# mLSTM outputs set aside in DRAM and the gate pairs woven into fewer column groups, in a hybrid encoder layer

## The chip, the cores and the metric

One Trainium2 chip, one core of it. The metric is the device time of one execution in microseconds, median of several runs. Times of single instructions come from one profiled execution.

## The reference

One layer over 256 rows of 2048 channels, float32: a SwiGLU feed-forward (2048 to 5632) with a residual and a layer norm; a mixer; a second feed-forward; a gated embedding. The change lies in the mixer:

```python
proj = x @ w_in                                   # 11272 columns
mq, mk, mv, mo, mi, mf, sq, sk, sv, ga, gb = _split_cols(proj)
q_m, k_m = split(silu(_causal_conv([mq, mk], conv_w)))
h   = _mlstm_chunkwise(q_m, k_m * 256**-0.5, mv, log_i, log_f)   # 4 heads of 256
y_m = head_norm(h) * sigmoid(mo)
y_sb = _stick_breaking(sq, sk, sv)                # 8 heads of 128
merged = sigmoid(ga) * (y_m @ w_up_m) + sigmoid(gb) * (y_sb @ w_up_sb)
return merged @ w_out
```

## The kernel before

**The work.** 256 rows are two halves `t` of 128. A product with a weight is cut into groups of 512 columns; a group runs over the weight's rows in pairs of 128. `group` makes one unit for each 256 rows of weight and each half `t`: six matmuls of 512 columns (L1194 to L1196), since each float32 operand is split into a high and a low part (hi x hi, hi x lo, lo x hi). So one weight tile is loaded once by the SP queue (`raw`, L1116), split once by ScalarE (high part, L1143) and VectorE (low part, L1147), and used by two units.

The pair of gates `ga` and `gb` is computed in another way. `seven` makes seven products in place of eight, Strassen's way, over sums of weight tiles: of each step of 512 rows a tile `t` is loaded, split, then grown by a DMA that adds another part of the weight to it (`grow`, L337, on GpSimd's queue), split again, and so on, until its fourth use; two more sums are made by VectorE (`plus`, L342). Here each split serves one unit only. `gates7(g)` makes such a group of four steps, 28 units, for each of the four column groups g; results are collected in two fixed banks, `seeded`.

**The order of the work.** Nothing is scheduled by a compiler: the program is a list of units, and `weave` puts the 28 x 4 = 112 units of the gates (with 20 blanks, `chained`) evenly between the units of `main`. Main holds the column groups of k, v, mo, q, k, v, mo (16 units each), six groups of stick-breaking columns (`sq0 + first * DS`, 16 units each, the last one of 256 columns), and six up halves of 8 units (`ups(g, half)`: half 0 is y_m times `w_up_m`, half 1 y_sb times `w_up_sb`, for g = 0, 1, 2): 256 units in all. The up products of g = 3 follow behind the weave.

Work that is no unit runs as a generator in `Sched`, put into the order after so many microseconds of planned TensorE time (`DELAY`): convolution, gate scans, the heads of mLSTM (`mlstm(h)`) and stick breaking (`stick(h)`), transposes (`sb_turn`), the derived forms of the activations that the seven products read (`form_turn`, with delay "form1" for the mixer's input).

**Memory.** One pool of 44 pages of 4 KB a partition serves raw tiles, split tiles, activations and most else. `room` holds two limits: how many raw tiles may be loaded and not yet free, and how many weights may be split ahead. Functions in main change it, `rooms(n)` the first alone, as the order reaches them; it begins at RAW_MIX = 8 and SPLIT_MIX = 4. A tile counts as raw until the last weight that is made of it has been split, for `t` of a pair its fourth. The output of mLSTM, transposed and split, is `ymT`: four tiles (head pair c, half t) of one page each, written by `split_psum` at the end of `mlstm` and read by the up products of half 0. They stay in their pages from the head that writes them until the last up product.

Of the kernel before, what the change touches and what calls it, by code (L numbers as in the profile page):

```python
# [13 lines left out]
P = 128  # L14
# [27 lines left out]


DELAY = {
    "gb": 12.0, "form": 14.0, "form1": 20.0, "ln_turn": 3.4, "ln_step": 1.2, "ln_low": 2.6, "h": 8.0, "silu": 6.0, "late": 9.0, "rest": 1.2, "mt": 3.2,
    "sbt": 4.6, "g0": 3.0, "g1": 4.0, "g2": 12.0, "cv0": 1.0, "cv1": 6.0, "turn": 3.5, "cv2": 1.3,
    "m0": 3.0, "m1": 0.6, "m2": 1.2, "m3": 4.6, "m4": 4.6, "s0": 6.6, "s1": 6.7, "s2": 4.0,
}

# [131 lines left out]
def kernel(  # L181
# [31 lines left out]
    def drop(n=1):  # L213
        temps[0] -= n
# [4 lines left out]
    def big(shape=(P, 1024)):  # L219
        return page_pool.tile(list(shape), F32, name="big", tag="page")  # L220

    pages, held, room = [0], [0], [RAW_MIX, SPLIT_MIX]

    def act_tile():
        pages[0] += 1
        return page_pool.tile([P, 2, 4, P], F32R, name="actT", tag="page")
# [163 lines left out]
    def rooms(*n):  # L390
        return lambda: room.__setitem__(slice(0, len(n)), n)
# [399 lines left out]
        return done  # L791

    ymT, ysbT = ActT(act_tile), ActT(act_tile)

    def diag(tl):
        return tl[:, 0:512].rearrange("q (a s) -> q a s", s=S)[:, :, 0:P]

    def mlstm(h):
        yield from wait("gates", ("qk", 0, h), ("qk", 1, h), ("v", 0, h // 2), ("v", 1, h // 2))
        d = temp()  # L800
        ps = misc([P, S])
        nc.tensor.matmul(ps[:], st["sel"][:, h], st["M"], start=True, stop=True)
        for s in range(2):
            activate(d[:, 256 * s:256 + P * s], ps[:, P * s:], ACT.Exp, scale=-1.0,
                                 bias=st["a"][:, s, h:h + 1])
        nc.gpsimd.affine_select(diag(d), diag(d), pattern=[[0, 2], [1, P]], compare_op=ALU.is_ge,
                                fill=0.0, base=0, channel_multiplier=-1)
        yield DELAY["m0"]
        q, k = st["qk", h][:, 0], st["qk", h][:, 1]
        ps = misc([P, 3 * P])  # L810
        for s in range(2):
            for b in range(2):
                nc.tensor.matmul(ps[:, 256 * s:256 + P * s], k[:, b, s * P:(s + 1) * P], q[:, b, s * P:],
                                 start=(b == 0), stop=(b == 1))
        nc.vector.scalar_tensor_tensor(out=d[:, 0:3 * P], in0=ps[:], scalar=DM ** -0.5, in1=d[:, 0:3 * P],
                                       op0=ALU.mult, op1=ALU.mult)
        yield DELAY["m1"]
        mv = small.tile([P, TT, 2], F32, name="hmv", tag="hmv")
        r = small.tile([P, TT], F32, name="hr", tag="hr")
        hs = temp().rearrange("q (t e) -> q t e", t=TT)  # L820
        for t in range(TT):
            ps = misc([P, DM + 1])
            for s in range(t + 1):
                off = s * 256 + (t - s) * P
                nc.tensor.matmul(ps[:], d[:, off:off + P], st["v", s, h // 2][:, h % 2], start=(s == 0), stop=(s == t))  # L825
            nc.vector.tensor_scalar(out=r[:, t:t + 1], in0=ps[:, DM:], scalar1=-1.0, scalar2=st["em"][:, t, h:h + 1],
                                    op0=ALU.mult, op1=ALU.max)
            nc.vector.tensor_tensor(out=r[:, t:t + 1], in0=ps[:, DM:], in1=r[:, t:t + 1], op=ALU.max)
            nc.vector.reciprocal(out=r[:, t:t + 1], in_=r[:, t:t + 1])
            yield DELAY["turn"]  # L830
            activate(hs[:, t], ps[:, 0:DM], ACT.Copy, scale=r[:, t:t + 1])
            yield DELAY["m2"]
        drop()
        for t in range(TT):
            stats = small.tile([P, 6], F32, name="hst", tag="hst")
            nc.vector.bn_stats(out=stats[:], in_=hs[:, t])
            nc.vector.bn_aggr(out=mv[:, t], in_=stats[:])
        rstd = small.tile([P, TT, 1], F32, name="hrs", tag="hrs")
        activate(rstd[:], mv[:, :, 1:2], ACT.Sqrt, bias=eps[:, 0:1])
        yield DELAY["m3"]  # L840
        yield from wait(("mo", 0, h // 2), ("mo", 1, h // 2))
        nc.vector.reciprocal(out=rstd[:], in_=rstd[:])
        for t in range(TT):
            nc.vector.tensor_scalar(out=hs[:, t], in0=hs[:, t], scalar1=mv[:, t, 0:1], scalar2=rstd[:, t],
                                    op0=ALU.subtract, op1=ALU.mult)
            nc.vector.tensor_tensor(out=hs[:, t], in0=hs[:, t], in1=st["mo", t][:, h * DM:(h + 1) * DM], op=ALU.mult)
        yield DELAY["m4"]
        for t in range(TT):
            ps = misc([P, 2, P])
            for b in range(2):  # L850
                nc.tensor.transpose(ps[:, b], hs[:, t, b * P:(b + 1) * P], ident[:])
            dst = ymT.get(h // 2, t)
            bs = slice(2 * (h % 2), 2 * (h % 2) + 2)
            split_psum(dst[:, 0, bs], dst[:, 1, bs], ps[:])
            ymT.mark(h // 2, t, 2)
        drop()

    def stick(h):
# [44 lines left out]
    head = group(w_in, range(0, D, 2 * P), 0, COL, x1T, qk_done(0, 0))  # L903
    program.extend(skewed(head[:SKEW]) + flat(head[SKEW:]))
    program.extend(columns(4096, 2 * HM + 2 * DS, gates_done))
    main = [rooms(10)] + columns(1024, COL, qk_done(1, 0)) + [rooms(8)]
    for g in range(2):
        if g:
            main += columns(COL, COL, qk_done(0, 1)) + [rooms(8)] + columns(1024 + COL, COL, qk_done(1, 1))
        else:  # L910
            main.append(load_norm_m)
        main += columns(2048 + g * COL, COL, v_done(g))
        main.append(lambda g=g: sched.spawn(in_sequence([mlstm(2 * g), mlstm(2 * g + 1)])))
        main += columns(3072 + g * COL, COL, mo_done(g))
    for first, n in ((2, 4), (8, 4), (16, 4), (12, 4), (20, 4), (6, 2)):
        main += columns(sq0 + first * DS, n * DS, lambda ps, t, f=first, n=n: sb_columns(ps, t, f, n))
        if first in (2, 20):
            main.append(rooms(11 if first == 2 else 6))
        if first == 16:
            main.append(rooms(8))  # L920
            main.append(lambda: [sched.spawn(in_sequence([stick(a), stick(a + 2), stick(a + 4), stick(a + 6)]))
                                 for a in (0, 1)])

# [55 lines left out]
    def merge_turn(g, t):  # L979
        transposed(gt[g, t], mergedT, g, t)  # L980
        return
        yield
# [3 lines left out]
            return flat(group(w_up_sb, range(0, HS * DS, 2 * P), g * COL, COL, ysbT, up_done(g, 1)))  # L986
        return flat(group(w_up_m, range(0, HM * DM, 2 * P), g * COL, COL, ymT, up_done(g, 0)))

    for half in range(2):
        for g in range(3):  # L990
            main += ups(g, half) + [rooms(8)]
    program.extend(weave(main, chained([gates7(g) for g in range(4)])))
    program.append(rooms(10, 6))
    program.append(lambda: [sched.spawn(merge_turn(g, t), 1.0 + 2.0 * g + t) for g in range(3) for t in range(TT)])
    program.append(lambda: sched.spawn(refill(), 14.0))
    program.extend(ups(3, 0) + ups(3, 1))
# [237 lines left out]
```

## Time and profile before

| | us |
|---|---|
| median of 3 runs (2218.99 to 2222.85) | 2220.16 |
| the profiled execution | 2221.91 |
| its span in the trace | 2220.2 |
| TensorE busy in the span | 2184.8 |
| VectorE, ScalarE, GpSimd busy | 1789.1, 1336.0, 228.8 |

The first feed-forward ends near 700 us, the mixer's woven part lies between about 740 and 1280, the second feed-forward and the embedding fill the rest. PE is TensorE, DVE VectorE, ACT ScalarE, POOL GpSimd, SP the queue that issues most loads. Matmuls are pipelined, so that a row lasts longer (0.39 us) than the distance from one start to the next (0.23 us). In a list of waits the columns are who waited for whom, microseconds in total, times, the longest.

### The profile page before, as it was taken

What the parts mean: (1) busy time and instruction counts of PE and PEld (TensorE: products, weight loads), DVE (VectorE), ACT (ScalarE), POOL (GpSimd) and SP (SyncE); (2) the same over time, 40 slices, a digit from 0 to 9 for tenths busy, and PEclk for the clock granted to TensorE, in tenths of its full rate; (3) what the DMA queues carried; (4) which work ended last, traced back from release to release, by engine and by line L of the source; (5) the groups of instructions that cost most, each with busy time, mean ns of one, the idle gap of its engine ahead of it and who ended that gap; (6) DMA issues with size and microseconds to landing.
All of it is one profiled execution on the core that took longest, in us unless ns stands there. A gap on an engine that the chain in (4) does not pass through costs nothing.

```text
span 2220.2 us, 27770 instructions
## 1 busy us (share of the span) xinstructions
PE 2184.8 (98%) x9972; PEld 1806.4 (81%) x9972; DVE 1789.1 (81%) x1967; ACT 1336.0 (60%) x1599; POOL 228.8 (10%) x201
## 2 busy tenths in 40 slices
PE   9999999999999999999998999999999999999999
PEld 7888888888887878778886888888888888888878
DVE  6889988888897878767655786599898989889884
ACT  6556656666575566665665554556665666666562
POOL 3111011110100011000111000011101110100000
PEclk9999999999999999999998999999999999999999
DMA  9899889987992878859575785579879998989652
GB/s 346 219 255 268 258 243 287 278 250 211 272 350 72 227 199 229 227 173 286 159 199 159 256 276 203 195 182 320 248 232 270 288 251 253 260 253 305 223 165 74
DMA packets 273194, 522.86 MB, mean 236 GB/s; under 512 B 16512, under 2 KB 25632, under 8 KB 272800
## 3 DMA queue, kind: packets, MB, share of 16 engines
q1 hardware_dynamic: 229248, 435.10, 57.9%
q0 software_dynamic: 43808, 85.99, 21.6%
q8 instruction: 78, 1.28, 0.2%
q14 instruction: 60, 0.49, 0.1%
HBM read 516.83 MB, written 4.19 MB: 235 GB/s over the span
## 4 chain that ended last, share of the span: by engine, by line
PE 92%; DVE 3%; ACT 2%; DMA 1%; issue 1%; DVEq 0%; SPq 0%; ACTq 0%
PE mm L1195 25%; PE mm L1196 25%; PE mm L1194 25%; PE seeded L1195 5%; PE seeded L1196 5%; PE seeded L1194 5%; DVE split L1147 2%; PE ms L267 1%; DMA raw<-in_w_in_dram 1%; ACT split L1143 1%; DMA raw<-in_w_up_m_dram 0%; PE ms L452 0%; PE ms L863 0%; PE ms L825 0%; DVE temp L761 0%
## 5 line engine op out<-in xcount | busy, mean ns | idle before, releaser
L1147 DVE TENSOR_TENSOR split<-raw,split 128x1024 fp32r<-128x1024 f32 (+2 forms) x1061 | 1242.7, 1205 | 221.2 <-ACT split L1143 208.0
L1143 ACT CAST split<-raw 128x1024 fp32r<-128x1024 f32 (+2 forms) x1061 | 1069.8, 1038 | 507.2 <-PE mm L1195 138.2
L1194 PE MATMUL mm<-split,actT 128*128 128x512 f32 (+2 forms) x2640 | 1027.9, 389 | 2.7 <-ACT big L1050 2.4
L1195 PE MATMUL mm<-split,actT 128*128 128x512 f32 (+2 forms) x2640 | 1017.1, 385 | 7.1 <-DVE split L1147 7.0
L1196 PE MATMUL mm<-split,actT 128*128 128x512 f32 (+2 forms) x2640 | 1016.7, 385 | 2.3 <-DVE actT L272 2.3
L1195 PEld LDWEIGHTS mm<-split,actT 128*128 128x128 f32 x2640 | 497.7, 189 | 106.8 <-DVE split L1147 11.6
L1196 PEld LDWEIGHTS mm<-split,actT 128*128 128x128 f32 x2640 | 497.0, 188 | 102.4 <-DVE actT L272 3.2
L1194 PEld LDWEIGHTS mm<-split,actT 128*128 128x128 f32 x2640 | 497.4, 188 | 100.1 <-ACT big L1050 3.3
L337 POOL DMA_DIRECT2D raw<-in_ffn_w_dram x128 | 154.7, 1219 | 1181.1 <-DVE split L1147 923.5
L342 DVE TENSOR_TENSOR raw<-raw 128x1024 f32<-128x1024 f32 x160 | 195.0, 1218 | 28.9 <-DMA raw<-in_w_in_dram 18.7
L1195 PE MATMUL seeded<-split,actT 128*128 128x512 f32 x480 | 187.9, 391 | 6.5 <-DVE split L1147 6.5
L1194 PE MATMUL seeded<-split,actT 128*128 128x512 f32 x480 | 189.1, 394 | 2.0 <-ACT split L1143 2.0
L1196 PE MATMUL seeded<-split,actT 128*128 128x512 f32 x480 | 187.5, 391 | 0.0
L568 DVE SCALAR_TENSOR_TENSOR xres<-mm,xres 128x512 f32<-128x512 f32 x160 | 108.9, 685 | 21.9 <-PE mm L1196 21.9
L1195 PEld LDWEIGHTS seeded<-split,actT 128*128 128x128 f32 x480 | 90.6, 189 | 25.9 <-DVE split L1147 7.9
L1194 PEld LDWEIGHTS seeded<-split,actT 128*128 128x128 f32 x480 | 90.4, 188 | 20.6 <-ACT split L1143 2.5
L1196 PEld LDWEIGHTS seeded<-split,actT 128*128 128x128 f32 x480 | 90.4, 188 | 18.9
L269 ACT CAST actT<-ms 128x512 fp32r<-128x512 f32 x60 | 35.2, 588 | 66.6 <-PE ms L267 65.0
L337 POOL DMA_DIRECT2D raw<-in_w_in_dram x32 | 38.7, 1208 | 310.5 <-DVE split L1147 302.7
L272 DVE TENSOR_TENSOR actT<-ms,actT 128x512 fp32r<-128x512 f32 x60 | 40.9, 685 | 24.7 <-ACT actT L269 14.3
L239 ACT ACTIVATE temp<-mm 128x512 f32<-128x512 f32 (+1 forms) x38 | 21.8, 574 | 57.9 <-PE mm L1196 57.8
L235 ACT ACT_TABLE_LOAD x35 | 44.9, 1283 | 0.6
(152 smaller groups left out, 706.8 us busy)
## 6 DMA issues: line engine op xcount, KB each, us to landing
raw<-in_ffn_w_dram SPq DMA_DIRECT2D x527, 512.0 KB, 8.1
raw<-in_w_in_dram SPq DMA_DIRECT2D x168, 512.0 KB, 4.8
raw<-in_ffn_w_dram POOLq DMA_DIRECT2D x128, 512.0 KB, 9.3
raw<-in_w_in_dram POOLq DMA_DIRECT2D x32, 512.0 KB, 7.7
raw<-in_w_out_dram SPq DMA_DIRECT2D x32, 512.0 KB, 5.8
raw<-in_w_ple_gate_dram SPq DMA_DIRECT2D x24, 512.0 KB, 4.9
raw<-in_w_up_m_dram SPq DMA_DIRECT2D x16, 512.0 KB, 5.4
raw<-in_w_up_sb_dram SPq DMA_DIRECT2D x16, 512.0 KB, 5.6
```

The source lines that it names most:

```text
L235: nc.scalar.preload_act_table_set(table[0])
L267: nc.tensor.transpose(ps[:, k], src[:, k * P:(k + 1) * P], ident[:])
L269: nc.scalar.copy(dst[:, 0], ps[:])
L272: nc.vector.tensor_tensor(out=dst[:, 1], in0=ps[:], in1=dst[:, 0], op=ALU.subtract)
L337: nc.gpsimd.dma_start(out=raw.tile[:, :, :cols], in_=src.src, accum_op=ALU.add)
L342: nc.vector.tensor_tensor(out=a.tile[:, :, :cols], in0=a.tile[:, :, :cols], in1=b.tile[:, :, :cols], op=ALU.add)
L568: nc.vector.scalar_tensor_tensor(out=xs, in0=ps, scalar=0.5, in1=xs, op0=ALU.mult, op1=ALU.add)
L1143: nc.scalar.copy(hi[:, ks], r[:, ks])
L1147: nc.vector.tensor_tensor(out=lo[:, ks], in0=r[:, ks], in1=hi[:, ks], op=ALU.subtract)
L1194: nc.tensor.matmul(ps, hi, w[0][:, k, :u.cols], start=first, stop=False, skip_group_check=u.onto)
L1195: nc.tensor.matmul(ps, hi, w[1][:, k, :u.cols], start=False, stop=False, skip_group_check=u.onto)
L1196: nc.tensor.matmul(ps, lo, w[0][:, k, :u.cols], start=False, stop=last, skip_group_check=u.onto)
```

## The change

It does four things.

1. **mLSTM's outputs go to DRAM.** When a tile of `ymT` has both its heads, `away(c, t)` stores it on GpSimd's queue (512 KB), after a delay of 6 us, and its page is given back. `back`, put into main four units ahead of the first up half, takes four new pages and loads the tiles again, on the same queue.
2. **The pairs are woven into less.** The three halves 1 of g = 0, 1, 2 leave main and follow behind the weave; main has 232 units in place of 256, among which the same 112 units of the pairs are spread.
3. **More raw tiles are loaded ahead** at most places of main, and six weights are split ahead in the head of the mixer in place of four (from the first unit of main on it is four again).
4. **Two delays:** the forms of the mixer's input come 10 us later ("form1"), the transposes of stick-breaking columns 1.4 us later ("sbt").

```diff
-    "gb": 12.0, "form": 14.0, "form1": 20.0, ...
-    "sbt": 4.6, ... "turn": 3.5, "cv2": 1.3,
+    "gb": 12.0, "form": 14.0, "form1": 30.0, ...
+    "sbt": 6.0, ... "turn": 3.5, "away": 6.0, "cv2": 1.3,
...
-    pages, held, room = [0], [0], [RAW_MIX, SPLIT_MIX]
+    pages, held, room = [0], [0], [RAW_MIX, 6]
...
+    aside = {(c, t): dram_pool.tile([P, 2, 4, P], F32R, name=f"aside{c}{t}") for c in range(2) for t in range(TT)}
+
+    def away(c, t):
+        nc.gpsimd.dma_start(out=aside[c, t][:], in_=ymT.tiles[c, t][:])
+        pages[0] -= 1
+        return
+        yield
+
+    def back():
+        for c in range(2):
+            for t in range(TT):
+                ymT.tiles[c, t] = act_tile()
+                nc.gpsimd.dma_start(out=ymT.tiles[c, t][:], in_=aside[c, t][:])
...
             ymT.mark(h // 2, t, 2)
+            if h % 2:
+                sched.spawn(away(h // 2, t), DELAY["away"])
...
-    main = [rooms(10)] + columns(1024, COL, qk_done(1, 0)) + [rooms(8)]
+    main = [rooms(10, 4)] + columns(1024, COL, qk_done(1, 0)) + [rooms(8)]
...
-            main += columns(COL, COL, qk_done(0, 1)) + [rooms(8)] + columns(1024 + COL, COL, qk_done(1, 1))
+            main += [rooms(9)] + columns(COL, COL, qk_done(0, 1)) + [rooms(9)] + columns(1024 + COL, COL, qk_done(1, 1))
...
         if first in (2, 20):
-            main.append(rooms(11 if first == 2 else 6))
+            main.append(rooms(12 if first == 2 else 10))
         if first == 16:
-            main.append(rooms(8))
+            main.append(rooms(11))
...
-    for half in range(2):
-        for g in range(3):
-            main += ups(g, half) + [rooms(8)]
+    main.insert(len(main) - 4, back)
+    for g in range(3):
+        main += ups(g, 0) + [rooms(12)]
     program.extend(weave(main, chained([gates7(g) for g in range(4)])))
     program.append(rooms(10, 6))
+    for g in range(3):
+        program.extend(ups(g, 1))
```

In the lists below, a line number of the changed kernel is 13 to 17 higher than that of the same statement before. Three places of the order:

The SP queue, at the loads of the last stick-breaking columns (`128x2x256`) and of the first up weights, before:

```order
L1116 DMA raw<-in_w_in_dram 128x2x512 x120
L1116 DMA raw<-in_w_in_dram 128x2x256
L1116 DMA raw<-in_w_in_dram 128x2x512 x2
L1116 DMA raw<-in_w_in_dram 128x2x256
L1116 DMA raw<-in_w_in_dram 128x2x512 x2
L1116 DMA raw<-in_w_in_dram 128x2x256 x2
L1116 DMA raw<-in_w_in_dram 128x2x512 x2
L1116 DMA raw<-in_w_in_dram 128x2x256 x4
L1116 DMA raw<-in_w_up_m_dram 128x2x512 x9
```

and now:

```order
L1133 DMA raw<-in_w_in_dram 128x2x512 x127
L1133 DMA raw<-in_w_in_dram 128x2x256 x6
L1133 DMA raw<-in_w_in_dram 128x2x512
L1133 DMA raw<-in_w_in_dram 128x2x256
L1133 DMA raw<-in_w_in_dram 128x2x512
L1133 DMA raw<-in_w_in_dram 128x2x256
L1133 DMA raw<-in_w_up_m_dram 128x2x512
L1133 DMA raw<-in_w_in_dram 128x2x512
L1133 DMA raw<-in_w_up_m_dram 128x2x512 x2
```

Loads of 512 columns of `w_in` are the pairs' there. Before, six of them stand among the eight narrow loads, and then nine up weights follow without one; now seven more of them stand ahead of the narrow loads, six narrow ones come in a row, and the pairs' loads alternate with the up weights.

GpSimd's queue between the last accumulating load of the mixer (L337) and the end of stick breaking, whose masks are the AFFINE_SELECT rows, before:

```order
L337 DMA raw<-in_w_in_dram 128x2x512 [waits DMASW4_49,DMASW0_49,DVE_49]
L881 AFFINE_SELECT temp<-temp 128x2x128 [waits Activation_49] x2
L337 DMA raw<-in_w_in_dram 128x2x512 [waits DMASW5_49,DMASW1_49,DVE_49]
L872 AFFINE_SELECT temp<-temp 128x2x128 [waits DVE_49,PE_49]
L872 AFFINE_SELECT temp<-temp 128x2x128 [waits DVE_49,PE_49,Activation_49]
```

and now:

```order
L337 DMA raw<-in_w_in_dram 128x2x512 [waits DMASW5_49,DMASW1_49,DVE_49]
L887 AFFINE_SELECT temp<-temp 128x2x128 [waits DVE_49,PE_49] x2
L806 DMA actT<-aside_94 128x1024 [waits DMAHW5_49,DVE_49,PE_49]
L806 DMA actT<-aside_95 128x1024 [waits DMAHW3_49,DMAHW5_49,DVE_49,Activation_49]
L806 DMA actT<-aside_96 128x1024 [waits DMAHW6_49,PE_49]
L806 DMA actT<-aside_97 128x1024 [waits PE_49]
L896 AFFINE_SELECT temp<-temp 128x2x128 [waits Activation_49] x2
```

The four reloads (L806) stand behind two masks that wait for VectorE, and two masks stand behind them. The DMASW and DMAHW names are semaphores of earlier DMAs.

TensorE at the end of the gates' columns (`128x264`) and at the first up half, before:

```order
L1196 MATMUL mm<-split,actT 128x264
L674 MATMUL ms<-ident,temp 128x128 [waits Activation_49]
L674 MATMUL ms<-ident,temp 128x128
L1194 MATMUL mm<-split,actT 128x512
L1195 MATMUL mm<-split,actT 128x512 [waits DVE_49]
```

and now, first the gates' end, then the first up half:

```order
L1213 MATMUL mm<-split,actT 128x264
L1211 MATMUL mm<-split,actT 128x512 [waits Activation_49]
...
L702 MATMUL ms<-ident,gst 4x128 [waits PE_49,Activation_49]
L702 MATMUL ms<-ident,gst 4x128 [waits Activation_49]
...
L1213 MATMUL mm<-split,actT 128x256
L1211 MATMUL mm<-split,actT 128x512 [waits Activation_49]
...
L1211 MATMUL mm<-split,actT 128x512 [waits DMASW6_49,PE_49,Activation_49]
...
L1211 MATMUL mm<-split,actT 128x512 [waits DMASW7_49,PE_49]
```

L674 is `sb_turn`, L702 the transposes of `gates`. Where the transposes stood right behind the gates' columns, 18 matmuls of 512 columns stand now, and the first thing of the gates that TensorE needs is `gst`. In the up half two units wait for the reloads (DMASW6 and DMASW7), six matmuls apart.

More of the change, by code (lines that the diff above doesn't have):

```diff
@@ L44 @@
 DELAY = {
-    "gb": 12.0, "form": 14.0, "form1": 20.0, "ln_turn": 3.4, "ln_step": 1.2, "ln_low": 2.6, "h": 8.0, "silu": 6.0, "late": 9.0, "rest": 1.2, "mt": 3.2,
-    "sbt": 4.6, "g0": 3.0, "g1": 4.0, "g2": 12.0, "cv0": 1.0, "cv1": 6.0, "turn": 3.5, "cv2": 1.3,
+    "gb": 12.0, "form": 14.0, "form1": 30.0, "ln_turn": 3.4, "ln_step": 1.2, "ln_low": 2.6, "h": 8.0, "silu": 6.0, "late": 9.0, "rest": 1.2, "mt": 3.2,
+    "sbt": 6.0, "g0": 3.0, "g1": 4.0, "g2": 12.0, "cv0": 1.0, "cv1": 6.0, "turn": 3.5, "away": 6.0, "cv2": 1.3,
     "m0": 3.0, "m1": 0.6, "m2": 1.2, "m3": 4.6, "m4": 4.6, "s0": 6.6, "s1": 6.7, "s2": 4.0,
```

## The prediction

> **What bounds the kernel now.** I read the page first: the busy times and the chain that ended last.
>
> ```profile
> PE 2184.8 (98%) x9972; PEld 1806.4 (81%) x9972; DVE 1789.1 (81%) x1967; ACT 1336.0 (60%) x1599; POOL 228.8 (10%) x201
> PE 92%; DVE 3%; ACT 2%; DMA 1%; issue 1%; DVEq 0%; SPq 0%; ACTq 0%
> ```
>
> TensorE is busy for 2184.8 of 2220.2 us and carries 92% of the chain. The change removes no matmul, so it can only win where TensorE stands idle (35.4 us in all) or runs slowly after standing idle. Where that is, the windows tell (columns: length, busy time of PE, PEld, DVE, ACT and POOL, granted clock, DMA share, GB/s):
>
> ```profile
> 0.00:700.00 700.00, 694.79 (x3119) 574.06 (x3120) 601.72 (x615) 429.11 (x475) 91.65 (x79) 1.00 0.88 261
> 725.00:750.00 25.00, 22.27 (x142) 20.04 (x141) 18.49 (x33) 16.07 (x27) 2.41 (x2) 0.93 0.82 225
> 750.00:1150.00 400.00, 393.23 (x1770) 320.91 (x1768) 296.86 (x373) 252.01 (x314) 45.78 (x43) 1.00 0.75 212
> 1150.00:1175.00 25.00, 20.66 (x95) 17.42 (x94) 12.31 (x13) 13.80 (x21) 1.21 (x1) 0.86 0.54 136
> 1175.00:1200.00 25.00, 22.03 (x132) 18.86 (x130) 16.16 (x19) 15.82 (x21) 7.12 (x8) 1.00 0.71 182
> 1200.00:1225.00 25.00, 20.50 (x82) 15.94 (x82) 13.08 (x18) 12.44 (x21) 1.68 (x2) 0.86 0.57 156
> ```
>
> Before 700 us, idle time is 5.2 us in 700. The three windows from 1150 to 1225, the last stick-breaking columns and the first up half, have 4.34 + 2.97 + 4.50 = 11.8 us idle in 75, and in two of them the clock is down to 0.86. DVE and ACT are *less* busy there than elsewhere, and the DMA engines too: nobody is short of throughput, everybody waits for one thing. The chain of waits of that stretch (start, length, what) names it:
>
> ```profile
> 1158.82 7.21 DMA raw<-in_w_in_dram
> ...
> 1168.57 0.80 PE seeded L1195
> 1169.37 0.43 PE seeded L1196
> 1169.79 0.43 PE seeded L1194
> ...
> 1173.92 4.93 DMA raw<-in_w_in_dram
> 1178.98 1.23 DVE raw L342
> ...
> 1196.19 10.43 DMA raw<-in_w_up_m_dram
> 1206.69 1.06 ACT split L1143
> ```
>
> All three stalls begin with a raw weight tile that was asked for too late. The groups of the mixer say how late is late (issue to landing, median):
>
> ```profile
> raw<-in_w_in_dram SPq DMA_DIRECT2D x164, 512.0 KB, 4.8
> raw<-in_w_in_dram POOLq DMA_DIRECT2D x32, 512.0 KB, 7.7
> raw<-in_w_up_m_dram SPq DMA_DIRECT2D x12, 512.0 KB, 6.5
> raw<-in_w_up_sb_dram SPq DMA_DIRECT2D x8, 512.0 KB, 6.1
> raw<-in_w_in_dram SPq DMA_DIRECT2D x8, 264.0 KB, 2.8
> ...
> kept<-xres POOLq DMA_DIRECT2D x2, 1024.0 KB, 5.6
> raw<-in_w_in_dram SPq DMA_DIRECT2D x8, 256.0 KB, 4.6
> ```
>
> How far ahead the loads run follows from `room`. These rows are of 640 to 1260 us, in which the SP queue loads 164 + 12 + 8 + 8 + 8 = 200 raw tiles of the mixer, one in 3.1 us. A seven-product group of four steps keeps its four `t` tiles from product 1 to product 4, and they count as raw. Where `rooms(6)` holds, behind the columns of `first == 20`, two places are left for all else: 2 x 3.1 = 6.2 us of lead, less than the 6.5 us that an up weight takes in the median and than the 7.21 and 10.43 us of the chain.
>
> **The change part by part.** *Rooms (term A).* Behind the same columns the limit is 10 and then 12 in place of 6 and 8: six to eight free places, 19 to 25 us of lead, more than 10.43. The order agrees: loads of the narrow last columns no longer alternate with the pair's. So the stalls of 1150 to 1225 should nearly go; what is late next there is the reload of term R. Their price is the idle 11.8 us plus what the slow clock costs. After a gap matmuls start 0.42 us apart (1169.37 to 1169.79), at full clock 0.23:
>
> ```profile
> 1139.97 0.39 PE L1194 MATMUL mm<-split,actT 128*128 128x512 f32 x1
> 1140.20 0.39 PE L1195 MATMUL mm<-split,actT 128*128 128x512 f32 x1
> ...
> 1161.28 0.28 PE L1196 MATMUL mm<-split,actT 128*128 128x256 f32 x1
> 1161.40 0.28 PE L1194 MATMUL mm<-split,actT 128*128 128x256 f32 x1
> ```
>
> A clock of 0.86 over 25 us is a shortfall of 3.5 us of full speed, 7.0 for two windows, part of it inside the idle time. So A is worth 11.8 to 18.8 us; I take 17 as what is there, since the slow pitch shows beyond the gaps, and 16 as what goes, leaving 1 for small waits that stay. The unfavourable end is 9: that only the two stalls of 1158 to 1183 go (idle 4.34 + 2.97, and half the clock's 3.5).
>
> *Seven-product units packed denser (no term).* 132 side places go over 232 units of main where they went over 256. With the two split rows and the sum row
>
> ```profile
> L1147 DVE TENSOR_TENSOR split<-raw,split 128x1024 fp32r<-128x1024 f32 (+2 forms) x1061 | 1242.7, 1205 | 221.2 <-ACT split L1143 208.0
> L1143 ACT CAST split<-raw 128x1024 fp32r<-128x1024 f32 (+2 forms) x1061 | 1069.8, 1038 | 507.2 <-PE mm L1195 138.2
> L342 DVE TENSOR_TENSOR raw<-raw 128x1024 f32<-128x1024 f32 x160 | 195.0, 1218 | 28.9 <-DMA raw<-in_w_in_dram 18.7
> ```
>
> a seven's unit asks DVE for 1.205 + 2/7 x 1.218 = 1.55 us per 6 x 0.23 = 1.38 us of TensorE, a main unit for half a split, 0.60. Before: (112 x 1.55 + 256 x 0.60) / (368 x 1.38) = 64%; after: (112 x 1.55 + 232 x 0.60) / (344 x 1.38) = 66%, and the last three up halves, which now run alone behind the weave, 44%. TensorE covers that; the up halves' own loads keep their place in SP's queue ahead of the last group's and cost nothing. What is lost is chance: 400 us of this weave have 6.8 us of idle (393.23 busy), each from a local pile-up that now falls elsewhere. I take 0, with ends -3 and +5.
>
> *Split depth 6 in the head, form1 30, sbt 6 (term C).* At 741 us TensorE stood 2.43 us, waiting for ScalarE to copy the gates' columns out, and the clock then fell:
>
> ```profile
> 743.83 0.69 PE L674 MATMUL ms<-ident,temp 128*128 128x128 f32 x2 [2.43 <-ACT temp L668]
> 744.17 0.78 PE L1194 MATMUL mm<-split,actT 128*128 128x512 f32 x1
> 744.74 0.63 PE L1195 MATMUL mm<-split,actT 128*128 128x512 f32 x1
> 745.17 0.63 PE L1196 MATMUL mm<-split,actT 128*128 128x512 f32 x1
> ```
>
> ScalarE was late because VectorE's convolution had the forms in front of it, four instructions between
>
> ```profile
> 737.88 0.42 DVE L291 TENSOR_TENSOR temp<-big 128x256 f32<-128x256 f32 x1
> ...
> 739.01 0.42 DVE L294 SCALAR_TENSOR_TENSOR temp<-big,temp 128x256 f32<-128x256 f32 x1
> ```
>
> The forms now come 10 us later, and by the order TensorE does 18 matmuls, 4.1 us, before it needs the copy: more than 2.43. The window's price is 2.7 idle plus up to 1.75 of clock. I take -2.5, with ends 0 (the forms' 1.7 us of DVE delays another split) and -4.5. The Trainium skill (TensorE: Matmul & The Clock Gate, "Part 1: The HAM clock gate") has the clock fall after about 3.4 us of idleness, by which a gap of 2.43 would cost only itself and C would end at -2.7; the rows above show the slow pitch of 0.43 us behind it, so the trace decides and I count the clock for short gaps too.
>
> *Stores and reloads (term R).* `away` adds four DMAs of 512 KB and `back` four, all on GpSimd's queue, each issue between 0.56 us (a 128-descriptor store of this shape's kind) and 1.21:
>
> ```profile
> L607 POOL DMA_DIRECT2D kept<-xres x2: 563/586/608, 809.6 to 813.0; - x2
> L337 POOL DMA_DIRECT2D raw<-in_w_in_dram x32 | 38.7, 1208 | 310.5 <-DVE split L1147 302.7
> ```
>
> At most 10 us on an engine that is 10% busy. Behind `away` wait the accumulating loads of `grow`; they wait for VectorE's splits anyway, and their consumers stand a whole product later, so I cost the stores at nothing; without that cover one issue, 1.2 us, would be late per store. The 8 x 0.52 = 4.2 MB meet DMA engines that are 75% busy. The reloads are different: TensorE waits for them. They stand four main units of 256 columns before the first up half, 4 x 6 x 0.12 = 2.9 us, and two or three pair units between, 2.8 to 4.1: 5.7 to 7.0 us of lead for a DMA that lands in 5.6 (the 1 MB store) to 7.7 us (the accumulating loads). That is a stall of nothing to 2.0; the worst landing in that place was 10.43, which makes 4.7, and with the 1.75 of slow clock of term C some 6.5. I take +1.5, ends 0 and +6.5.
>
> Sum: -16 - 2.5 + 0 + 1.5 = -17. The profiled execution took 2221.9 us around a span of 2220.2; -17 makes 2204.9. The median of the runs is 2220.16, 1.75 below the profiled one; the same -17 makes **2203 us**.
>
> **The rivals.**
> 1. *The limit was not room but pages.* 44 pages are shared; with `rooms(12)` a load may wait for a page instead. For it: SP's longest waits are for TensorE to let go of a tile, in the whole kernel
>
> ```profile
> SPq L1116 <- PE mm L1196: 965.4, 373, 18.4
> ```
>
> Against: four pages of ymT are free for most of the time. Then A is -9, C 0, R +1.5: -7.5, or 2212.7.
> 2. *Descriptors starved.* The reloads come late because GpSimd's DMAs do: its loads land at 7.7 us where SP's land at 4.8. The reload then costs 7.7 - 5.7 = 2.0 of stall and 1.75 of slow clock, 3.8 in place of 1.5: -14.7, or 2205.5. The Trainium skill (SBUF — State Buffer, "Who interferes with whom") says that a VectorE instruction holding the shared port shuts GpSimd out until it ends, which speaks against reloading on this queue. The 2.9 us between the two rows go that way, though part of them is the addition that these loads make.
> 3. *Stalls move.* A goes down by 9, and the pile-ups of the denser weave (+5) and the reload (+3) take most of it back: -1, or 2219. For it: the weave's idle time has no single cause.
> 4. *The reload is stuck in GpSimd's queue (slower).* Ahead of the reloads stand two selects that wait for VectorE, and GpSimd has waited long for such:
>
> ```profile
> POOL temp L872 <- DVE temp L871: 48.7, 2, 24.6
> ```
>
> If VectorE comes to them 24.6 us late, the first up half waits that long at the one place that I counted as won: 24.6 - 5.7 = 18.9 of stall and 3.5 of clock. It lies on the third stall of term A, so that of A only 9 is won: -9 - 2.5 + 22.4 = +10.9, or 2231. It decides from about 13.7 us of lateness on (8 of stall), and makes the kernel slower by 0.2% from 18 us on. Against it: a waiting GpSimd had mostly nothing due, so a wait of 24.6 is not 24.6 of lateness.
>
> **How the numbers follow.** Forecast 0.50, rival 1 0.16, rival 2 0.12, rival 3 0.12, rival 4 0.10. No change means within 0.2%, 4.4 us, about what a measurement of this kernel can tell: 2215.7 to 2224.6. Forecast and rivals 1 and 2 are faster: 0.78; rival 3 is the same, 0.12; rival 4 slower, 0.10. For the range, the favourable ends A -18.8, C -4.5, weave -3, R 0 would make 2194; above, rival 1 with a reload of +5 makes 2216. Rivals 3 and 4 lie mostly outside, 0.2. Range 2194 to 2217.
>
> **What would show it.** Right: in the windows around the last stick-breaking columns TensorE busy above 24 of 25 with clock 1.00, and no raw DMA at the head of a stall there; no wait of L674 for the copy after the gates; the first up half waiting under 3 us for the reload. Wrong: idle time there as before (rival 1), a wait of 5 us or more on the reload (2, 4), or more than 12 us of idle in the weave before it (3).

## The result and the profile after

| | us |
|---|---|
| before, median of 4 runs beside those of after (2218.99 to 2222.85) | 2220.76 |
| after, median of 4 runs (2207.95 to 2209.66) | 2208.25 |
| ratio, 95% interval | 0.9945, 0.9927 to 0.9962 |
| after, the profiled execution and its span | 2208.55, 2206.8 |

The change makes the kernel 12.5 us faster, 0.55%. The forecast was 2203, 17 us faster, with 2194 to 2217 as the range: right in sign and range, 5 us too hopeful. The sum hides that at least two of its four terms came out outside their ends, in opposite directions; that it landed so near is in part luck.

The page's busy times of after:

```profile
PE 2182.0 (99%) x9972; PEld 1805.6 (82%) x9972; DVE 1789.7 (81%) x1967; ACT 1334.4 (60%) x1600; POOL 233.0 (11%) x209
```

TensorE's idle time fell from 35.4 to 2206.8 - 2182.0 = 24.8 us; the other 2.8 of the span's 13.4 us are a shorter busy time of the same 9972 matmuls. Between 640 and 1260 us the granted clock stood at one half for 17.1 us in before and for 13.7 in after. The windows of the prediction, of after (busy times of PE, PEld, DVE, ACT, POOL, then granted clock, DMA share, GB/s):

```profile
0.00:700.00 700.00, 694.99 (x3126) 574.33 (x3127) 602.60 (x617) 430.06 (x477) 91.36 (x79) 1.00 0.88 261
725.00:750.00 25.00, 25.00 (x165) 22.70 (x164) 18.70 (x31) 17.16 (x27) 4.80 (x4) 1.00 0.91 257
750.00:1150.00 400.00, 394.73 (x1765) 322.03 (x1764) 306.39 (x379) 253.24 (x317) 46.58 (x47) 1.00 0.80 225
1150.00:1175.00 25.00, 22.90 (x119) 19.45 (x117) 11.23 (x15) 17.18 (x29) 3.92 (x4) 1.00 0.79 167
1175.00:1200.00 25.00, 24.24 (x126) 21.06 (x126) 18.82 (x22) 14.50 (x21) 4.42 (x8) 0.86 0.67 222
1200.00:1225.00 25.00, 22.57 (x98) 18.33 (x98) 17.46 (x23) 14.54 (x23) 2.10 (x2) 0.93 0.80 281
```

From 1150 to 1225 the idle time went from 11.8 to 2.10 + 0.76 + 2.43 = 5.3 us, and two of the three windows still have a slow clock. At 725 to 750 nothing is idle any more; 750 to 1150, the weave, has 5.3 us idle where it had 6.8. What TensorE still waits for between 700 and 1260 (who for whom: total, times, longest):

```profile
PE mm L1212 <- DVE split L1164: 2.7, 4, 1.3
PE ms L878 <- DVE big L680: 2.4, 1, 2.4
PE seeded L1211 <- ACT split L1160: 2.1, 1, 2.1
PE seeded L1212 <- DVE split L1164: 2.0, 2, 1.2
...
```

Leaving small ones aside, there are three places, none headed by a load. First the v columns near 780 us, which had only 1.1 us of idle time before, from 775 to 800 (timeline of TensorE):

```profile
780.40 0.49 PE L1211 MATMUL mm<-split,actT 128*128 128x512 f32 x1 [1.44 <-ACT split L1160]
782.15 0.50 PE L1212 MATMUL mm<-split,actT 128*128 128x512 f32 x1 [1.26 <-DVE split L1164]
...
783.24 0.63 PE L1212 MATMUL mm<-split,actT 128*128 128x512 f32 x1
783.66 0.63 PE L1213 MATMUL mm<-split,actT 128*128 128x512 f32 x1
```

Second 1172 us, on TensorE and then on ScalarE:

```profile
1174.62 0.50 PE L1211 MATMUL seeded<-split,actT 128*128 128x512 f32 x1 [2.10 <-ACT split L1160]
1175.88 0.79 PE L1212 MATMUL seeded<-split,actT 128*128 128x512 f32 x1 [0.76 <-DVE split L1164]
1176.47 0.63 PE L1213 MATMUL seeded<-split,actT 128*128 128x512 f32 x1
1176.90 0.63 PE L1211 MATMUL seeded<-split,actT 128*128 128x512 f32 x1
```

```profile
1168.32 0.87 ACT L239 ACTIVATE temp<-ms 128x384 f32<-128x384 f32 x2
1169.21 1.28 ACT L235 ACT_TABLE_LOAD   x1
...
1171.58 0.85 ACT L239 ACTIVATE temp<-ms 128x384 f32<-128x384 f32 x2
...
1173.02 0.61 ACT L239 ACTIVATE temp<-temp,ones 128x384 f32<-128x384 f32 x1
1173.54 3.02 ACT L1160 CAST split<-raw 128x1024 fp32r<-128x1024 f32 x4
```

From 1168.32 to 1173.54 ScalarE computes the exponentials and logarithms of two stick-breaking heads, one behind the other, with a table load between; only then come the splits. Third 1205 us, TensorE and VectorE:

```profile
1207.80 1.57 PE L878 MATMUL ms<-big 128*128 128x256 f32 x8 [2.43 <-DVE big L680]
```

```profile
1204.73 1.22 DVE L342 TENSOR_TENSOR raw<-raw 128x1024 f32<-128x1024 f32 x1
1205.86 1.22 DVE L1164 TENSOR_TENSOR split<-raw,split 128x1024 fp32r<-128x1024 f32 x1
1207.00 0.75 DVE L680 COPY big<-ms 128x256 f32<-128x256 f32 x2
```

The copies of the last stick-breaking columns stand behind a sum row and a split.

### The profile page after: what moved, and what is told of

Read it like the earlier page. It is cut to its first block, busy times and chain, and to the rows that moved or that the text cites. A ratio compares the mean times of both kernels' runs of the same rounds, so it can differ in the third digit from the quotient of the medians.

```text
span 2206.8 us, 27786 instructions
## 1 busy us (share of the span) xinstructions
PE 2182.0 (99%) x9972; PEld 1805.6 (82%) x9972; DVE 1789.7 (81%) x1967; ACT 1334.4 (60%) x1600; POOL 233.0 (11%) x209
## 4 chain that ended last, share of the span: by engine, by line
PE 93%; DVE 2%; ACT 2%; DMA 1%; issue 1%; DVEq 0%; ACTq 0%
PE mm L1212 25%; PE mm L1213 25%; PE mm L1211 25%; PE seeded L1212 5%; PE seeded L1213 5%; PE seeded L1211 5%; DMA raw<-in_ffn_w_dram 1%; DVE split L1164 1%; PE ms L267 1%; ACT split L1160 1%; PE ms L452 0%; ACT temp L239 0%; PE ms L838 0%; PE ms L891 0%; PE ms L878 0%
## 5 line engine op out<-in xcount | busy, mean ns | idle before, releaser
L1164 DVE TENSOR_TENSOR split<-raw,split 128x1024 fp32r<-128x1024 f32 (+2 forms) x1061 | 1241.6, 1205 | 220.5 <-ACT split L1160 200.0
L337 POOL DMA_DIRECT2D raw<-in_ffn_w_dram x128 | 153.9, 1216 | 1171.0 <-DVE split L1164 971.0
L337 POOL DMA_DIRECT2D raw<-in_w_in_dram x32 | 38.6, 1211 | 335.6 <-DVE split L1164 308.1
L272 DVE TENSOR_TENSOR actT<-ms,actT 128x512 fp32r<-128x512 f32 x60 | 41.0, 685 | 24.8 <-ACT actT L269 15.5
```

The source lines that it names most:

```text
L272: nc.vector.tensor_tensor(out=dst[:, 1], in0=ps[:], in1=dst[:, 0], op=ALU.subtract)
L337: nc.gpsimd.dma_start(out=raw.tile[:, :, :cols], in_=src.src, accum_op=ALU.add)
L1164: nc.vector.tensor_tensor(out=lo[:, ks], in0=r[:, ks], in1=hi[:, ks], op=ALU.subtract)
```

## The experiments

All times are medians beside runs of before on the same chip (2220.1 to 2220.8); a ratio is to before, with its 95% interval. The theory at the start was the prediction's, that late raw loads were the price and the limits (`rooms`) the cure; the rivals were that the weave, or the pages, did it.

**The head's edits alone.** These are the delays and the split depth (item 4 of the change and the second half of item 3); "head" is the start of the mixer here, no head of attention.

```diff
-    "form1": 20.0, ... "sbt": 4.6,
+    "form1": 30.0, ... "sbt": 6.0,
-    pages, held, room = [0], [0], [RAW_MIX, SPLIT_MIX]
+    pages, held, room = [0], [0], [RAW_MIX, 6]
-    main = [rooms(10)] + ...
+    main = [rooms(10, 4)] + ...
```

> The kernel before with only the head's edits: split depth 6 in the mixer's head, form1 30, sbt 6; weave, rooms of the rest and ymT as before. Theory (the late raw loads of 1150 to 1225 were the change's main price, the head's stall only moved): the wait of sb_turn for ScalarE at 741 us goes (2.7 us of idle), a new one comes at the first v columns near 780 us (about 3 us), the stalls of 1150 to 1225 stay at 11 to 12 us of idle: 2218 to 2222 us, within 0.2% of before. Rival (the head's edits give what the forecast gave them, -2.5, or more): 2214 to 2218.

2225.32 us, ratio 1.0020 (1.0011 to 1.0029): slower than before by 4.5, more than either side expected. The wait at 741 us is gone and the v columns pay for it, here in two windows:

```profile
725.00:750.00 25.00, 25.00 (x165) 22.72 (x164) 17.79 (x29) 15.73 (x25) 4.07 (x4) 1.00 0.91 269
775.00:800.00 25.00, 20.29 (x80) 15.27 (x80) 22.59 (x32) 15.93 (x21) 4.82 (x4) 0.93 0.66 142
```

4.7 us are idle at 775 to 800, where after has 3.0 and before 1.1 us. The wait for the copies of the last stick-breaking columns grew too, from 1.0 us in before (L863) to 2.6.

**Two limits alone.**

```diff
-            main.append(rooms(11 if first == 2 else 6))
+            main.append(rooms(11 if first == 2 else 8))
-            main += ups(g, half) + [rooms(8)]
+            main += ups(g, half) + [rooms(10)]
```

> The kernel before with two numbers changed: rooms(8) in place of 6 behind the columns of first == 20, rooms(10) in place of 8 behind each up half. Weave, delays and ymT stay. Theory (lead of the raw loads): two places more are 6 us more lead, 12 in all, above the 10.43 us of the worst load; the three stalls of 1158 to 1206 lose most of their 11.8 us of idle without any store, reload or new weave: 2207 to 2213 us. Rival (it is the weave, with three halves moved out, that feeds the stretch): 2218 to 2222.

2213.63 us, ratio 0.9969 (0.9957 to 0.9981): 7.2 us won by two numbers, just above the theory's range and far from the rival's. Two of the three stalls headed by loads went. The first stayed, with 4.47 us of wait at 1169 us and a load at its head (chain of waits):

```profile
1159.25 7.41 DMA raw<-in_w_in_dram
...
1169.19 0.79 PE seeded L1195
```

**Fewer places in after.**

```diff
-            main.append(rooms(12 if first == 2 else 10))
+            main.append(rooms(12 if first == 2 else 7))
-            main.append(rooms(11))
+            main.append(rooms(8))
-        main += ups(g, 0) + [rooms(12)]
+        main += ups(g, 0) + [rooms(7)]
```

> The kernel after with fewer places for raw tiles from the last stick-breaking columns on: rooms(7) in place of 10 at first == 20, 8 in place of 11 at first == 16, 7 in place of 12 behind the up halves. Stores, reloads, the new weave and the delays stay. Theory (lead): three free places, 9 us, are about what a load takes there, so a part of the stalls comes back, 4 to 8 us, and a raw load heads a stall again: 2212 to 2217 us. Rival (the weave gives it, or the pages): the time stays at 2208, with no load at the head of a stall.

2207.53 us, ratio 0.9942 (0.9929 to 0.9955): as after, and no load heads a stall. The theory missed. It is the rival's case. With the new weave and the pages of `ymT` free, a limit of 7 or 8 lets the loads through as well as 10 to 12. That limits of 6 and 8 were too low in the old weave is shown by the run before this one; that they had to be doubled is not.

**After without stores and reloads.**

```diff
-            if h % 2:
-                sched.spawn(away(h // 2, t), DELAY["away"])
-    main.insert(len(main) - 4, back)
```

> The kernel after without the stores and reloads of ymT: its four pages are held until the up projections, all else as after. Theory (lead by rooms; the pages are not short): the loads run as far ahead as before, 2206 to 2209 us, within 0.1% of after. Rival (the pages are the limit, and setting ymT aside is what lets the loads run ahead): stalls of 1150 to 1225 headed by raw loads come back, 2213 to 2219.

2216.13 us, ratio 0.9978 (0.9969 to 0.9988): the rival on pages has the time, but not the picture. No load heads a stall; instead the splits of the two engines take turns. One of ScalarE's waits from 1125 to 1215, of this run, of after, and of the new weave alone with its limit of 8 (below), which keeps `ymT` in its pages too:

```profile
ACT split L1157 <- DVE split L1161: 14.4, 10, 2.7
```

```profile
ACT split L1160 <- DVE split L1164: 2.9, 2, 1.7
```

```profile
ACT split L1144 <- DVE split L1148: 2.3, 1, 2.3
```

A wait of ScalarE's split for VectorE's split fits a pool of pages that is empty, where the next split needs the page of a raw tile that VectorE has just read for the last time. That reading is an argument from one row. The third line says what empties the pool: with `ymT` kept but the limits low the wait is 2.3 us, so it seems to take the higher limits and the kept pages together.

**A square of weave and `ymT`.** Three more kernels. The new weave alone, against before, with the limit of 8 of the second experiment (behind the up halves it keeps 8, where that experiment has 10):

```diff
-            main.append(rooms(11 if first == 2 else 6))
+            main.append(rooms(11 if first == 2 else 8))
-    for half in range(2):
-        for g in range(3):
-            main += ups(g, half) + [rooms(8)]
+    for g in range(3):
+        main += ups(g, 0) + [rooms(8)]
     program.extend(weave(main, chained([gates7(g) for g in range(4)])))
     program.append(rooms(10, 6))
+    for g in range(3):
+        program.extend(ups(g, 1))
```

> The kernel before with the new weave (three up halves behind it) and rooms(8) in place of 6 at first == 20; ymT stays in its pages, delays as before. With the run that changed only the limits (2213.6 us), the run of after without the stores (2216.1) and the next two, a square of weave by ymT. Theory (pages: the denser weave keeps more tiles at once, and needs the four pages of ymT): stalls spread over 1100 to 1200 as in after without the stores, 2213 to 2218 us, no better than the limits alone. Rival (the new weave by itself is worth what the limits do not explain): 2206 to 2210.

The stores and reloads in the old weave, against the second experiment:

```diff
+            if h % 2:
+                sched.spawn(away(h // 2, t), DELAY["away"])
+    main.insert(len(main) - 4, back)
     for half in range(2):
         for g in range(3):
             main += ups(g, half) + [rooms(10)]
```

> The kernel before with the two limits (8 and 10) and with ymT's stores and reloads, the reloads four units ahead of the first up half; old weave with all six halves, old delays. Theory (pages): four pages more let the loads and splits of 1150 to 1215 run ahead there too; against the limits alone (2213.6) it gains 3 to 7 us, 2206 to 2211. Rival (only the denser weave is short of pages, the old one was not): within 2 us of 2213.6.

And after with the head's edits undone:

```diff
-    "form1": 30.0, ... "sbt": 6.0,
+    "form1": 20.0, ... "sbt": 4.6,
-    pages, held, room = [0], [0], [RAW_MIX, 6]
+    pages, held, room = [0], [0], [RAW_MIX, SPLIT_MIX]
```

> The kernel after with the head's edits undone: form1 20, sbt 4.6, split depth 4 in the head. Theory (they cost: with before they made it 4.5 us slower, moving the stall of 741 us to the first v columns and making it longer): the wait at 741 comes back with 2.7 us of idle, the one of 780 us goes, 2204 to 2207 us, faster than after. Rival (the forecast's term C, -2.5): 2210 to 2212, slower than after.

| limits raised, and | us | ratio, interval |
|---|---|---|
| old weave, ymT kept | 2213.63 | 0.9969 (0.9957 to 0.9981) |
| old weave, ymT stored | 2218.14 | 0.9986 (0.9978 to 0.9995) |
| new weave, ymT kept (limit 8) | 2208.50 | 0.9945 (0.9933 to 0.9958) |
| new weave, ymT stored (limits of after) | 2204.79 | 0.9929 (0.9917 to 0.9942) |

The square is not a clean one: the last row has the higher limits of after as well. The new weave by itself is worth 5.1 us, the rival's case; the theory on pages fell for it. Undoing the head's edits gave 3.5 us, the theory's case. The windows of the second experiment, and of the new weave alone, show where the weave's gain comes from:

```profile
800.00:1100.00 300.00, 295.19 (x1315) 240.78 (x1314) 212.96 (x264) 190.51 (x230) 28.09 (x27) 0.99 0.75 214
1100.00:1150.00 50.00, 50.00 (x232) 40.82 (x231) 36.22 (x40) 31.15 (x44) 10.61 (x11) 1.00 0.76 213
1150.00:1225.00 75.00, 68.72 (x345) 57.56 (x344) 46.42 (x56) 45.55 (x67) 10.27 (x11) 0.95 0.74 200
```

```profile
800.00:1100.00 300.00, 297.53 (x1336) 243.80 (x1335) 221.22 (x269) 189.44 (x231) 29.32 (x27) 1.00 0.79 228
1100.00:1150.00 50.00, 47.66 (x215) 37.64 (x214) 37.20 (x40) 31.34 (x42) 9.20 (x9) 1.00 0.71 190
1150.00:1225.00 75.00, 71.59 (x369) 60.67 (x368) 50.75 (x61) 53.13 (x78) 9.96 (x12) 1.00 0.75 207
```

Idle time falls by 2.3 us at 800 to 1100 and by 2.9 at 1150 to 1225, rises by 2.3 between, and the clock rises in two of the three. The largest piece is the stall at 1169 us that a late load headed: its 4.47 us are gone, no load heads a stall there, and TensorE's longest wait from 1100 to 1230 is now

```profile
PE seeded L1195 <- ACT split L1144: 2.1, 1, 2.1
```

The clock in these windows flatters the weave: the profiled execution (2206.87 us) is the fastest of its five, and the only one with a mean clock of 1.000; the other four have 0.998 and took 2208.16 to 2209.34.

Storing `ymT` costs 4.5 us in the old weave, which neither side expected; in the new one, storing it and raising the limits to those of after win 3.7 together. What each does there can be estimated, if the head's edits cost their 3.5 us in every kernel of the new weave. Without stores, the limits of after make 2216.1 - 3.5 = 2212.6, against 2208.5 with the limit of 8: raising them costs about 4 us. With stores, limits of 7 and 8 make 2207.5 - 3.5 = 2204.0, as good as the higher ones. So the stores are worth about 4.5 us at low limits, and raising the limits further wins nothing.

In the old weave the gap on the raw load goes (24.66 of 25 us busy at 1150 to 1175, where the limits alone have 20.53), and the reload takes its place (this execution is the slowest of its eleven):

```profile
1150.00:1175.00 25.00, 24.66 (x133) 21.16 (x132) 15.72 (x20) 17.07 (x28) 1.23 (x1) 1.00 0.78 207
1175.00:1200.00 25.00, 17.57 (x98) 14.95 (x97) 14.94 (x16) 13.72 (x18) 10.32 (x12) 0.85 1.00 274
```

```profile
1197.48 0.76 PE L1211 MATMUL mm<-split,actT 128*128 128x512 f32 x1 [7.43 <-DMA actT<-aside]
```

```profile
L807 POOL DMA_DIRECT2D actT<-aside x4: 1031/1048/1070, 1186.1 to 1187.7; - x4
...
DMA to landing us min/median/max: 11.3/13.5/15.5
```

The reloads were issued from 1186.1 us on, behind three accumulating loads that had waited for VectorE's splits, and TensorE needed the first at 1190. This is the wait that the prediction's term R feared and its fourth rival placed in GpSimd's queue, in the kernel without the new weave; it came behind the accumulating loads and not, as that rival had it, behind the masks. At 800 to 1100 us this kernel has 2.0 us more idle time than the limits alone, too (293.23 against 295.19 us busy).

**Staggered heads**, against the stall at 1172 us.

```diff
-                                 for a in (0, 1)])
+                                 for a in (0,)])
+            main.append(lambda: sched.spawn(in_sequence([stick(a) for a in (1, 3, 5, 7)]), 6.0))
```

> The kernel after with the second chain of stick-breaking heads begun 6 us after the first (before they began together). Theory (what is left of the stall at 1172 us is ScalarE's work of two heads, whose exponentials and logarithms come at the same time ahead of the splits): the wait of 2.1 us on ScalarE's split there and the slow pitch behind it go, 2204 to 2207 us. Rival (the heads are a chain of their own and the second one then ends too late): TensorE waits for the last head before the next up halves, 2208 to 2213.

2207.46 us, ratio 0.9940 (0.9927 to 0.9954): between the two cases, and hardly apart from after (runs of 2205.98 to 2208.67). The wait on ScalarE's split shrank from 2.10 to 0.83 us and the next one, on VectorE's, stayed at 0.76:

```profile
1175.92 0.49 PE L1212 MATMUL seeded<-split,actT 128*128 128x512 f32 x1 [0.83 <-ACT split L1161]
1177.18 0.50 PE L1213 MATMUL seeded<-split,actT 128*128 128x512 f32 x1 [0.76 <-DVE split L1165]
```

ScalarE's two heads at once were the cause of 1.3 of the 2.1 us; their whole price is unclear at this size.

**Two pages fewer in after** (`PAGES = 42` in place of 44).

> The kernel after with 42 pages in place of 44, all else as after. Theory (what the limits of 10 to 12 need is pages; storing ymT gives four of them, so that without it after became 7.9 us slower): half of those four are gone again, and stalls of 1100 to 1185 come back in part, with ScalarE's splits waiting for VectorE to let go of raw tiles: 2210 to 2215 us. Rival (pages are not what bound the kernel without the stores): 2208, as after.

2223.35 us, ratio 1.0014 (1.0005 to 1.0023): 15 us slower than after, but not where expected. The edit also does more than was meant: outside the mixer, `loads` compares the pages in use with `PAGES - SPARE`, so that the feed-forwards load less far ahead as well. The first 700 us, and the same two waits as in after, in this run:

```profile
0.00:700.00 700.00, 688.86 (x3070) 568.12 (x3071) 595.45 (x603) 423.61 (x461) 90.89 (x79) 1.00 0.87 258
```

```profile
791.16 0.50 PE L1211 MATMUL mm<-split,actT 128*128 128x512 f32 x1 [1.42 <-ACT split L1160]
...
1220.87 1.44 PE L878 MATMUL ms<-big 128*128 128x256 f32 x3 [2.43 <-DVE big L680]
```

They come 791.16 - 780.40 = 10.8 and 1220.87 - 1207.80 = 13.1 us later than in after. So 10.8 us were lost ahead of 780, 694.99 - 688.86 = 6.1 of them as idle time before 700, then 2.3 us up to 1207; the rest of the 17.3 us between the two profiled executions comes later. The stalls expected at 1100 to 1185 did not come. Two pages do not bind the last stretch of the mixer; whether the four of `ymT` do, at the limits of after, stays open.

**sbt alone undone in after** (`"sbt": 4.6`; form1 30 and depth 6 stay).

> The kernel after with sbt 4.6 in place of 6.0; form1 30 and depth 6 stay. Theory (of the head's edits' 3.5 us, the part at 1205 us is sbt's: VectorE's copies of the last stick-breaking columns fell behind an addition and a split there): the wait of 2.4 us on the copies goes, with the slow pitch behind it, 2204.5 to 2206.5 us; the stall near 780 stays. Rival (form1 and the depth alone cost it): 2208.

2205.14 us, ratio 0.9938 (0.9924 to 0.9952), all runs from 2204.40 to 2207.15, below after's 2207.95 to 2209.66: the theory's case. The intervals of the two ratios overlap, so the trace has to bear it out, and it does: the wait of L878 is gone, and the second copy of L680 comes ahead of the sum row and the split (1205.73 us, before 1206.06 and 1207.19), where in after it comes behind them. By the medians, 3.1 of the 3.5 us that the head's edits cost in after are the 1.4 us of sbt. form1 and depth 6 together cost the rest, 0.4 us, which is no more than noise: the stall of 741 us became that of 780.

**The forms earlier in place of later**, after with the head's edits undone and

```diff
-    "form1": 20.0,
+    "form1": 0.0,
```

> The kernel after with the head's edits undone (2204.8 us) and the forms 20 us earlier than before the change, form1 0. Theory (VectorE works without a pause from 729 to 790 us and stood idle 7.4 us ahead of that: the change moved the forms the wrong way, into the full stretch): most of the forms' 12 us fall into the pause, the small stalls of 780 to 812 go, and the wait at 741 shrinks by what no longer stands ahead of it: 2201 to 2204 us. Rival (the pause is needed by the first splits and the convolution, which the forms would now delay): TensorE waits at 730 us, 2206 to 2210.

2200.12 us, ratio 0.9912 (0.9898 to 0.9926): the theory's case, better than expected, 4.7 us below the kernel without this edit. In before VectorE has one long pause ahead of the first convolution:

```profile
729.55 0.71 DVE L1147 TENSOR_TENSOR split<-raw,split 128x528 fp32r<-128x528 f32 x1 [7.42 <-ACT split L1143]
```

With the forms in it, 700 to 800 us (after, then this run) has more of VectorE's work done and less idle TensorE; the stalls at 741 and at 780 are both gone:

```profile
700.00:800.00 100.00, 95.84 (x477) 79.60 (x475) 84.03 (x128) 64.86 (x103) 9.57 (x8) 0.98 0.68 182
```

```profile
700.00:800.00 100.00, 97.89 (x499) 82.49 (x497) 87.64 (x134) 66.68 (x108) 9.54 (x8) 1.00 0.71 192
```

**Both together**, the forms early and the heads staggered.

> The kernel with the forms early (2200.1 us: after with sbt 4.6, depth 4 and form1 0), and the second chain of stick-breaking heads begun 6 us after the first. Theory (ScalarE's two heads at once are the largest stall left, 2.26 us of excess at 1169 us and some 5 with what follows; alone in after the same edit won 0.8, since a part came back at 1106 and 1175): 2198 to 2200 us. Rival (the wait only moves to the next split): 2200 to 2202, no faster.

2198.41 us (2197.66 to 2200.38), ratio 0.9904 (0.9888 to 0.9921): the fastest kernel here, 22 us below before and 10 below after. Against the forms alone (2198.71 to 2200.47) the stagger's 1.7 us is at the edge of what the runs tell apart.

## Why the prediction was right, and where it was not

The 12.5 us of the change as steps, each the difference of two kernels that were run: two limits -7.2, the new weave -5.1, storing `ymT` with the higher limits -3.7, the head's edits +3.5 (in all -12.5). The order of the steps matters, as the square shows: stored in the old weave, `ymT` costs 4.5. The forecast's -17 and this sum lie close by luck as well: the weave's 5.1 us, forecast as 0, hide most of what C lost, 6.0 us from -2.5 to +3.5. Of the prediction's own signs of being right, no load at the head of a stall, no wait of L674 at the gates and no wait for the reload came true; a TensorE busy above 24 of 25 us at clock 1.00 did not (22.90, 24.24 and 22.57 us, at 1.00, 0.86 and 0.93).

- **Term A, -16 forecast, -7.2 measured by two limits alone, -10.9 with the step that raised them further and stored `ymT`.** The mechanism was right: the raw loads' lead was too short, two limits remove two of the three stalls, and no load heads a stall in after. The size was off. The step that failed is "so the stalls of 1150 to 1225 should nearly go", put down to the limits: the first of the three stayed with 4.47 us when two limits were raised in the old weave, and went with the new weave at a limit of 8. Whether a higher limit ahead of it would have done the same in the old weave was not run. "16 as what goes, leaving 1 for small waits that stay" failed as well: 2.10 + 0.76 us stayed, for ScalarE's two heads were next in line behind the late load, with slow matmuls behind them (the other 2.43 us that after has idle there are sbt's, in term C). And "six to eight free places, 19 to 25 us of lead" were not what was needed: limits of 7 and 8 do as well.
- **Weave, 0 forecast with ends -3 and +5, -5.1 measured.** Outside its ends. The argument from VectorE's average load (64% to 66%) said nothing about which pile-ups would go; "a local pile-up that now falls elsewhere" failed, since fewer fell than before; the largest that went was a stall that the prediction had counted in A.
- **Term C, -2.5 forecast with ends 0 and -4.5, +3.5 measured.** The wrong sign. The stall at 741 went, as forecast. The step that failed is to price the delays by that stall alone: VectorE has work from there to 790 us with no pause above 0.75 us, so that ten microseconds later meant into a full stretch; and sbt, which the forecast had in C's name and gave no price, cost 3.1 us (by the medians) at the other end of the mixer. The prediction's end of 0 named "another split" and stopped there.
- **Term R, +1.5 forecast, no wait in after.** No run has the reloads alone, so this is read from the trace: no row has TensorE waiting for a reload, though they landed in 9.4 us in the median, above the 5.6 to 7.7 that the forecast counted with:

```profile
L806 POOL DMA_DIRECT2D actT<-aside x4: 538/554/587, 1189.5 to 1191.2; - x4
...
DMA to landing us min/median/max: 7.3/9.4/11.6
```

  The lead was therefore longer than the forecast's 5.7 to 7.0 us. In the old weave the same edit cost 7.4 us of wait. The Trainium skill (DMA: Bandwidth & Descriptors, "Anatomy of one DMA — SWDGE (gpsimd) path") fits such a DMA as 2.0 us plus its bytes over 436 GB/s, an estimate of 3.2 us for 512 KB; four issued in a row took 7.3 to 11.6 us here and 11.3 to 15.5 in the old weave, so the measurement decides.
- **The rivals.** Rival 3, stalls that move, is what happened to C. Rival 1, pages, holds in part: without the stores after is 7.9 us slower. Rival 2's slow landings are there (9.4 us) and cost nothing in after. Rival 4's wait is real in one kernel of the square; in after GpSimd waited 6.8 us ahead of the reloads, but for a load and not for VectorE, and TensorE did not feel it.

## What to carry to other kernels

Before a piece of work is delayed, look for the pause of its engine on both sides of it: here the same work moved 10 us later won nothing, and 20 us earlier, into a pause of 7.4 us, it won 4.7. When a late load heads a stall, ask what is late next at that place, and price only the difference. A raised limit takes its memory from something: the last raise here cost about 4 us (an estimate) where `ymT` kept its pages, and won nothing where they were free. And give each delay that a change touches a term of its own; the one without a price was the one that cost most.

## What the runs showed of the hardware

- The clock fell behind some gaps of 2 to 2.5 us and not behind others of the same length. At 743 us TensorE waits for the same copy in before (2.43 us, in the prediction's rows) and in the run of the new weave alone (2.42 us). Of the latter, the wait and the window around it (length, busy time of PE, PEld, DVE, ACT and POOL, granted clock, DMA share, GB/s):

```profile
PE ms L674 <- ACT temp L668: 2.4, 1, 2.4
```

```profile
725.00:750.00 25.00, 22.27 (x151) 20.11 (x150) 19.06 (x34) 16.95 (x28) 2.41 (x2) 1.00 0.82 221
```

  Before has the same 22.27 us of busy time in this window, at a clock of 0.93 and with 142 matmuls in place of 151: from 743.68 on the clock is granted by half for 3.41 us.
  So too near 1175 us: behind gaps of 2.10 and 0.76 us matmuls of 512 columns start 0.43 us apart in after (1176.47 to 1176.90) and 0.23 us apart in the new weave alone (1180.31 to 1180.54). Between the first and the last 20 us of these traces, the stretches at half clock last 3.41, 6.83 or 10.24 us, whole multiples of 3.41. What decides whether one begins, the runs do not show. By an estimate from these rows, each 3.41 us at half clock loses up to 1.7 us, so that much of a difference between two executions can be chance.
- One and the same reload was issued in 0.54 to 0.59 us in after and in 1.03 to 1.07 us in the old weave, and of the four stores in after two took 0.58 to 0.60 and two 1.05 to 1.07; the runs do not show why.
